# One transformer layer in split fp32: moving the casts of the first feed-forward's up projection, loading the condition row earlier, and keeping two pieces of its down projection

## The chip, the core and the metric

The kernel runs on one core of one Trainium2 chip. The metric is the device time of one execution in microseconds (us), as the median of several runs. Five engines work side by side, each with its own instruction queue: TensorE (PE in the profile; PEld is its weight load), VectorE (DVE), ScalarE (ACT), GpSimd (POOL), and SyncE (SP), which here only issues DMAs. GpSimd issues DMAs too, and a DMA in its queue that has to wait holds back everything behind it.

## The reference, cut to what is computed

Two streams of 256 tokens with 2048 channels: the latent tokens `x` and the context tokens `ctx`. A layer is a SwiGLU half step on both streams, a mixing step (attention of grouped queries beside a Hyena convolution), and a second SwiGLU half step on the latent stream. Each is preceded by an RMS norm with shift, scale and gate from a condition vector through one linear map `w_ada`.

```python
mod   = (silu(c)     @ w_ada + b_ada)[:, None, :]
mod_c = (silu(c_ctx) @ w_ada + b_ada)[:, None, :]

def swiglu(h, w_up, w_down):
    gate, up = split(h @ w_up, 2, axis=-1)
    return (silu(gate) * up) @ w_down          # w_up: 2048 x 11264, w_down: 5632 x 2048

def half_ffn(s, m, slot, g, w_up, w_down):
    h = modulate(rms_norm(s, g), chunk(m, 3 * slot), chunk(m, 3 * slot + 1))
    return s + 0.5 * chunk(m, 3 * slot + 2) * swiglu(h, w_up, w_down)

x   = half_ffn(x,   mod,   0, g_norm[0], w_ffn1_up, w_ffn1_down)
ctx = half_ffn(ctx, mod_c, 0, g_norm[0], w_ffn1_up, w_ffn1_down)
# then: projections of both streams, keys and values first; attention, Hyena, output projection
x   = half_ffn(x, mod, 2, g_norm[2], w_ffn2_up, w_ffn2_down)
```

All data are fp32.

## The kernel before

**Split products.** Every fp32 operand is kept as a high part `hi` (a rounded copy, made by a cast on ScalarE) and a remainder `lo = x - hi` (a subtraction on VectorE). A product is three TensorE instructions, hi·hi, hi·lo and lo·hi (`mm3`, L247 to L249). Weights come in pieces of 512 KB, `raw` tiles with four buffers (`weight_load`, L224); `weight` makes `whi` (cast, L236) and `wlo` (L240), three buffers each.

**The wave.** The first three of the 44 tiles (of 128 columns of gate and 128 of value) of the up projection run side by side while the channels d = 0 to 15 are normalised one after the other (`wave_h`, L872 to L876). Into the same stretch go the rows of `w_ada` for the first shift and scale (`wrow` loads by SyncE, products L190), and the steps of the Hyena filter, whose results `spec` GpSimd stores (L726). Then the three tiles are closed (`close`, L381 is the silu), the condition row goes through GpSimd into a small tile (L955), through silu (L959) and back to memory (L960), and SyncE spreads it over all partitions (`crow`, L968).

**The up projection, tiles j = 3 to 43 (`up`, L490).** Both streams go through at once, 512 columns a product. A tile has four pieces, kq = 0 to 3, of 512 KB. Piece 0 is always "plain": its two halves are cast (L425), the negated high part is written (L426), and the raw piece is added to it by an accumulating DMA on GpSimd's queue (L427), so that VectorE has no part in it; it is loaded by GpSimd (L224) into a pool of one buffer, `plain`. From j = 5 piece 3, from j = 7 piece 2 and from j = 9 piece 1 are "quads": in place of 16 products there are 14 of half the width, of sums of weights and sums of activations. Such a piece is prepared one piece ahead, in this order: cast `bhi` of its plain blocks (ACT, L436), remainder `blo` (DVE, L439), three sums in `raw` (DVE, L442 to L444), cast `whi` of the sums (ACT, L465), remainder `wlo` (DVE, L471). `bhi` and `blo` have two buffers.

**The close of a tile with quads (L516 to L524).** ScalarE copies a part out of PSUM (L516), VectorE forms six sums, ScalarE takes silu (L523), VectorE multiplies (L524), giving the act `u`. Then ScalarE casts the act (L534) and writes the negative (L535), and GpSimd stores both (L536, L537) and later accumulates the act on the second (L270, which is the line of the helper `then`). PSUM banks alternate between PA and PB by tile, so that the next tile starts while one is closed.

**Dots.** The rest of `w_ada` is applied on VectorE as dot products of 1.28 us (L151) of 512 KB loads `adaw` (L141 and L144, SyncE, two buffers) with `crow`. After every piece a hook adds the rate 0.82 to an account and issues a dot for each whole one; hooks start at j = 4.

**The down projection.** Eleven groups of four tiles, in two passes of four pieces dq. The last two groups of the second pass run by halves (`APART`): first the context half (part 1), then the latent half (part 0), both with all pieces dq = 4 to 7 loaded and split; while the latent half runs, the context stream is normalised on VectorE and ScalarE (L342 to L345), and each finished piece is added to the stream (L584). Then comes the projection to keys and values (L1055 to L1057), whose weights go through L236 and L240.

**What sets the order.** The instruction streams are made by a scheduler that follows the order of the code and priorities; `then` and `issue_after` put one instruction behind another in that order.

Of the kernel before, what the change touches and what calls it, by code (L numbers as in the profile page):

```python
# [18 lines left out]
P = 128  # L19
D = 2048  # L20
# [14 lines left out]
ADA_RATES = (0.82, 1.15, 1.42)  # L35
# [27 lines left out]
def hybrid_layer_kernel(ctx: ExitStack, tc: tile.TileContext, a):  # L63
# [296 lines left out]
    class Ffn:  # L360
        def __init__(self, wup, wdown, cm, hook=None):
# [4 lines left out]
            self.held = {}  # L366
            self.sums, self.first, self.begun, self.unadded = {}, {}, None, None
# [50 lines left out]
        def prepare(self, j, kq):  # L418

            pool = adap if kq == 0 and j > WAVE else None  # L420
            raw = weight_load(self.wupq[j - WAVE, kq], (P, 2, 4, P), nc.gpsimd if pool else None, pool)
            if kq == 0:
                hi, lo = ([U((P, 4, P), F32R) for _ in range(2)] for _ in range(2))
                for q in range(2):
                    S.copy(hi[q], raw[:, q])  # L425
                    S.activation(lo[q], hi[q].bitcast(F32), AF.Copy, scale=-1.0)  # L426
                    self.added = nc.gpsimd.dma_start(lo[q], raw[:, q].bitcast(F32R), accum_op=ALU.add)  # L427
                return [(hi, lo)]
            if not self.quads(j, kq):
                return [weight(None, (P, 2, 4, P), raw=raw)]  # L430
            return raw

# [13 lines left out]
        def quad_weights(self, j, kq):  # L446
# [15 lines left out]
            with ExitStack() as order:  # L462
                if cast is not None:
                    order.enter_context(tc.issue_after(cast.ins))
                S.copy(thi, raw)  # L465
# [24 lines left out]
        def up(self, j):  # L490
# [4 lines left out]
            for kq in range(4):  # L495
                w = self.ahead if kq == 0 else self.quad_weights(j, kq) if self.quads(j, kq) else self.prepare(j, kq)
# [30 lines left out]
        def keep(self, j, act):  # L527
# [5 lines left out]
            hi, minus = U((P, 2, L), F32R), U((P, 2, L), F32R)  # L533
            S.copy(hi, act)  # L534
            S.activation(minus, hi.bitcast(F32), AF.Copy, scale=-1.0)  # L535
            nc.gpsimd.dma_start(actd[j][:, 0], hi)  # L536
            nc.gpsimd.dma_start(actd[j][:, 1], minus)  # L537
            self.unadded = j, act
            if j < WAVE:
                self.add_act()  # L540

        def add_act(self):
            if self.unadded:
                j, act = self.unadded
                self.unadded = None
                then(self.added, nc.gpsimd.dma_start, actd[j][:, 1], act.bitcast(F32R), accum_op=ALU.add)
# [16 lines left out]

        def step(self, g, dq, banks, begin, end, part=None, done_=None):
# [387 lines left out]
    for _ in steps:  # L952
        pass
# [729 lines left out]
```

## Time and profile before

| | |
|---|---|
| median of 3 runs | 2630.1 us |
| lowest and highest run | 2628.18, 2631.96 us |
| the profiled execution | 2625.92 us |
| its span | 2624.1 us |
| first close of the wave's tiles (L381) | 150.72 us |
| last close of the up projection (L516) | 1017.61 us |
| second wait of the key/value projection ends (L1056) | 1508.07 us |
| bytes read from HBM, written | 545.10 MB, 38.57 MB |
| mean granted clock of TensorE | 0.997 |

A row of the timeline gives the start, the duration, the engine, the line, the operation, output and inputs, their shapes, and in square brackets the idle time of the engine ahead of it with what ended it. Names without numbers stand for all tiles of that name. Matmuls overlap, so the distance between two starts is their price, not the duration: 0.227 us for 512 columns without a stall. A line number is one of the kernel before unless it is said otherwise.

### The profile page before, as it was taken

To read this page: it belongs to the slowest core of one execution; us is meant where nothing else is said; L and a number is where in the kernel's file an instruction comes from. 1 tells how busy PE (TensorE), PEld (TensorE's weight loads), DVE (VectorE), ACT (ScalarE), POOL (GpSimd) and SP (SyncE) were. 2 spreads that over 40 slices of the span, in tenths; PEclk is the share of its full clock that TensorE was granted. 3 is DMA by queue.
4 is the path that set the end of the run, shared out by engine and by line. 5 is a ranking of instruction groups with operands and counts; after the bars stand their busy time and mean duration, and the time that the engine had idled before them with its cause. 6 is when DMAs were issued, how large, how long until landed. Compare 5 with 4: busy or idle time off the path is not lost.

```text
span 2624.1 us, 38011 instructions
## 1 busy us (share of the span) xinstructions
PE 2592.5 (99%) x14480; PEld 2228.7 (85%) x14480; DVE 1891.7 (72%) x3051; ACT 1115.3 (43%) x1543; POOL 275.2 (10%) x435
## 2 busy tenths in 40 slices
PE   8999999999999999999999999999999999999999
PEld 5678999999999999888888988888788888888887
DVE  6766888888888887777988796888755455554444
ACT  5344444444444443112211555466544444444333
POOL 1121111212212123320010000000000000000000
PEclk9999999999999999999999999999999999999999
DMA  9987888888988889996897566345566555566665
GB/s 368 363 248 220 236 251 246 241 243 240 248 244 256 249 244 316 395 363 208 280 331 241 179 192 186 113 131 175 167 187 191 187 190 189 189 189 208 201 203 154
DMA packets 193925, 607.68 MB, mean 232 GB/s; under 512 B 22316, under 2 KB 25357, under 8 KB 189389
## 3 DMA queue, kind: packets, MB, share of 16 engines
q1 hardware_dynamic: 134684, 483.42, 56.3%
q0 software_dynamic: 58864, 121.69, 17.6%
q8 instruction: 113, 1.85, 0.3%
q14 instruction: 72, 0.58, 0.1%
q10 hardware_dynamic: 192, 0.13, 0.0%
HBM read 545.10 MB, written 38.57 MB: 222 GB/s over the span
## 4 chain that ended last, share of the span: by engine, by line
PE 84%; DVE 6%; DMA 5%; ACT 3%; issue 2%; POOL 0%; SPq 0%; DVEq 0%; ACTq 0%; POOLq 0%
PE pa L1343 10%; PE pa L1342 10%; PE pa L1344 10%; PE pb L247 7%; PE pb L249 7%; PE pb L248 7%; PE pa L247 7%; PE pa L249 7%; PE pa L248 7%; PE pa L255 3%; DMA adaw<-in_w_adaT_dram 2%; PE pa L257 2%; DVE wlo L471 1%; PE pa L1056 1%; PE pa L1057 1%
## 5 line engine op out<-in xcount | busy, mean ns | idle before, releaser
L240 DVE TENSOR_TENSOR wlo<-raw,whi 128x1024 fp32r<-128x1024 f32 x487 | 595.6, 1223 | 476.4 <-ACT whi L236 474.9
L236 ACT CAST whi<-raw 128x1024 fp32r<-128x1024 f32 x487 | 512.4, 1052 | 876.8 <-PE pa L1344 413.4
L1342 PE MATMUL pa<-whi,u 128*128 128x512 f32 x1060 | 413.9, 391 | 0.0
L1343 PE MATMUL pa<-wlo,u 128*128 128x512 f32 x1060 | 412.8, 390 | 0.3 <-DVE wlo L240 0.3
L1344 PE MATMUL pa<-whi,u 128*128 128x512 f32 x1060 | 412.8, 390 | 0.0
L247 PE MATMUL pa<-u,whi 128*128 128x256 f32 (+1 forms) x928 | 311.6, 337 | 2.2 <-ACT u L859 2.1
L249 PE MATMUL pa<-u,wlo 128*128 128x256 f32 (+1 forms) x928 | 309.5, 334 | 2.8 <-DVE wlo L471 2.8
L248 PE MATMUL pa<-u,whi 128*128 128x256 f32 (+1 forms) x928 | 309.2, 333 | 0.4 <-DVE u L864 0.4
L249 PE MATMUL pb<-u,wlo 128*128 128x256 f32 (+1 forms) x920 | 303.6, 330 | 3.1 <-DVE wlo L471 3.1
L247 PE MATMUL pb<-u,whi 128*128 128x256 f32 (+1 forms) x920 | 304.6, 331 | 0.0
L248 PE MATMUL pb<-u,whi 128*128 128x256 f32 (+1 forms) x920 | 302.8, 329 | 0.0
L1343 PEld LDWEIGHTS pa<-wlo,u 128*128 128x128 f32 x1060 | 199.0, 188 | 41.5 <-DVE wlo L240 0.7
L1344 PEld LDWEIGHTS pa<-whi,u 128*128 128x128 f32 x1060 | 199.0, 188 | 41.5
L1342 PEld LDWEIGHTS pa<-whi,u 128*128 128x128 f32 x1060 | 199.0, 188 | 40.7
L151 DVE CUSTOM_DVE_ANT_0 adas<-adaw,crow,cond 128x1024 bf16<-128x1024 f32 x160 | 204.9, 1281 | 11.1 <-DMA adaw<-in_w_adaT_dram 9.4
L151 DVE CUSTOM_DVE_ANT_0 adas<-adaw,crow,mod 128x1024 bf16<-128x1024 f32 x160 | 205.0, 1281 | 7.2 <-DMA adaw<-in_w_adaT_dram 5.1
L247 PEld LDWEIGHTS pa<-u,whi 128*128 128x128 f32 x928 | 176.1, 190 | 25.1 <-issue 4.5
L249 PEld LDWEIGHTS pa<-u,wlo 128*128 128x128 f32 x928 | 176.3, 190 | 21.4 <-DVE wlo L471 4.2
L249 PEld LDWEIGHTS pb<-u,wlo 128*128 128x128 f32 x920 | 174.7, 190 | 20.4 <-DVE wlo L471 4.5
L248 PEld LDWEIGHTS pa<-u,whi 128*128 128x128 f32 x928 | 176.5, 190 | 17.5 <-DVE u L864 1.5
L247 PEld LDWEIGHTS pb<-u,whi 128*128 128x128 f32 x920 | 174.8, 190 | 17.5 <-issue 2.0
L248 PEld LDWEIGHTS pb<-u,whi 128*128 128x128 f32 x920 | 174.8, 190 | 15.8 <-issue 0.4
(357 smaller groups left out, 4654.7 us busy)
## 6 DMA issues: line engine op xcount, KB each, us to landing
adaw<-in_w_adaT_dram SPq DMA_DIRECT2D x224, 512.0 KB, 5.8
raw<-in_w_dn_dram SPq DMA_DIRECT2D x184, 512.0 KB, 4.3
raw<-in_w_up_dram SPq DMA_DIRECT2D x176, 512.0 KB, 3.5
raw<-in_w_up1q_dram SPq DMA_DIRECT2D x124, 512.0 KB, 5.0
u<-act POOLq DMA_DIRECT2D x136, 256.0 KB, 10.9
act<-u POOLq DMA_DIRECT2D x131, 256.0 KB, 5.0
wrow<-in_w_ada_dram SPq DMA_DIRECT2D x32, 1024.0 KB, 9.3
plain<-in_w_up1q_dram POOLq DMA_DIRECT2D x40, 512.0 KB, 6.3
```

The costliest lines, as they stand in the source:

```text
L151: V.tensor_tensor_reduce(out=sc, in0=t, in1=crow[i][:, b * (D // 2) : (b + 1) * (D // 2)], scale=1.0, scalar=mcol if b else bada[:, c * KT ...
L236: S.copy(hi, raw)
L240: last_lo[0] = V.tensor_sub(lo, raw, hi.bitcast(F32))
L247: PE.matmul(ps, w[0], xx[0], start=start, stop=False)
L248: PE.matmul(ps, w[0], xx[1], start=False, stop=False)
L249: return PE.matmul(ps, w[1], xx[0], start=False, stop=stop)
L255: PE.matmul(ps, w[0], x, start=start, stop=stop)
L257: PE.matmul(ps[:, 0, :], w[1], x[:, 0, :], start=False, stop=False)
L471: last_lo[0] = V.tensor_sub(tlo, raw, thi.bitcast(F32))
L1342: PE.matmul(ps[t], hi, w[0], start=start, stop=False)
L1343: PE.matmul(ps[t], hi, w[1], start=False, stop=False)
L1344: last = PE.matmul(ps[t], lo, w[0], start=False, stop=stop)
```

## The change

Three parts.

**1. Casts.** The load of the plain piece is issued one tile earlier, behind the accumulate of the half before it. Its two halves are cast and negated at pieces 1 and 2 of the tile before (`plain_half`), each behind that piece's cast `whi` (`behind_cast`). The act is no longer cast at the close but at piece 3 of the next tile (`store`), again behind that piece's `whi`, with all of its stores and its accumulate, in two tiles of a pool `sg` of three buffers. The acts of the wave are stored at pieces 0, 2 and 3 of tile 3.

**2. Condition row.** The row is loaded at d = 6 of the wave, goes through silu at d = 8, and is spread at d = 14. The hooks issue dots from j = 3 on, at 0.80 instead of 0.82. The loads of ScalarE's function tables rise from 11 to 13 in the program, both new ones in the wave.

**3. Kept pieces.** In the last group of the down projection, pieces dq = 6 and 7 are loaded once, in the context half, and split there in two halves each into general tiles (`U`); the latent half takes them from there.

```diff
-ADA_RATES = (0.82, 1.15, 1.42)
+ADA_RATES = (0.8, 1.15, 1.42)
...
         def prepare(self, j, kq):
-            pool = adap if kq == 0 and j > WAVE else None
-            raw = weight_load(self.wupq[j - WAVE, kq], (P, 2, 4, P), nc.gpsimd if pool else None, pool)
-            if kq == 0:
...
-                for q in range(2):
-                    S.copy(hi[q], raw[:, q])
-                    S.activation(lo[q], hi[q].bitcast(F32), AF.Copy, scale=-1.0)
-                    self.added = nc.gpsimd.dma_start(lo[q], raw[:, q].bitcast(F32R), accum_op=ALU.add)
+        def plain_half(self, j, q):
+            raw = self.plain[0]
+            if q == 0:
+                self.ahead = [tuple([U((P, 4, P), F32R) for _ in range(2)] for _ in range(2))]
+            hi, lo = self.ahead[0][0][q], self.ahead[0][1][q]
+            self.behind_cast(S.copy, hi, raw[:, q])
+            S.activation(lo, hi.bitcast(F32), AF.Copy, scale=-1.0)
+            nc.gpsimd.dma_start(lo, raw[:, q].bitcast(F32R), accum_op=ALU.add)
+            if q == 1 and j >= WAVE + 1:
+                self.plain_load(j + 1, adap)
+
+        def side(self, j, kq):
+            if kq in (1, 2) and j < JT - 1:
+                self.plain_half(j + 1, kq - 1)
+            if self.kept and (kq == 3 or j == WAVE and kq != 1 or j == JT - 1 and kq == 1):
+                self.store(*self.kept.pop(0))
...
-                if kq == 1:
-                    if j < JT - 1:
-                        self.ahead = self.prepare(j + 1, 0)
-                    self.add_act()
+                self.side(j, kq)
                 self.hook()
...
+        def store(self, j, act):
+            hi, minus = (T(up, (P, 2, L), "sg", F32R, 3) for _ in range(2))
+            self.behind_cast(S.copy, hi, act)
             S.activation(minus, hi.bitcast(F32), AF.Copy, scale=-1.0)
+            then(self.plain[1], nc.gpsimd.dma_start, actd[j][:, 0], hi)
             nc.gpsimd.dma_start(actd[j][:, 1], minus)
+            nc.gpsimd.dma_start(actd[j][:, 1], act.bitcast(F32R), accum_op=ALU.add)
...
+            if part is not None and end and dq in PASSES[-1][-2:]:
+                halves = self.kept_weight(g, dq)
+            else:
+                whi, wlo = weight(self.wdown[g, dq], (P, GRP, 2, P))
+                halves = [(whi[:, n : n + 2], wlo[:, n : n + 2]) for n in (0, 2)]
...
+        if d == 6:
+            rows = U((2 * KT, P))
+            nc.gpsimd.dma_start(rows, a["crow"].rearrange("i (k p) -> (i k) p", p=P))
+        if d == 8:
+            S.activation(rows, rows, AF.Silu)
+            nc.gpsimd.dma_start(silu_rows.rearrange("i k p -> (i k) p"), rows)
+        if d == KT - 2:
...
+            row_in(rows_pool, 0)
```

In the order of instructions the change shows at four places; line numbers are those of each kernel. First ScalarE at a close of the stage with quads. Before, around the close that begins with L516 (L534 and L535 are the act, L425 and L426 the plain halves, L436 and L465 the quads' bhi and whi):

```order
L516 COPY sq_3021<-pb_2805 128x256
L465 CAST whi_3076<-raw_2964 128x1024
L523 ACTIVATE sq_3021<-sq_3021 128x512
L534 CAST u_3033<-u_3022 128x512
L535 ACTIVATE u_3034<-u_3033 128x512
L425 CAST u_3128<-plain_3126 128x512
L436 CAST bhi_3145<-raw_3143 128x768
L426 ACTIVATE u_3130<-u_3128 128x512
L425 CAST u_3129<-plain_3126 128x512
L465 CAST whi_3148<-raw_3071 128x1024
L426 ACTIVATE u_3131<-u_3129 128x512
```

The same place now (L534 begins the close, L541 is its silu, L456 bhi, L485 whi; L270 on plain with L438 is a plain half, L270 on u with L557 the act):

```order
L534 COPY sq_2799<-pa_2581 128x256
L270 CAST u_2898<-plain_2714 128x512
L438 ACTIVATE u_2900<-u_2898 128x512
L541 ACTIVATE sq_2799<-sq_2799 128x512
L456 CAST bhi_2909<-raw_2907 128x768
L485 CAST whi_2912<-raw_2843 128x1024
L270 CAST u_2899<-plain_2714 128x512
L438 ACTIVATE u_2901<-u_2899 128x512
L456 CAST bhi_2971<-raw_2969 128x768
L485 CAST whi_2974<-raw_2907 128x1024
L270 CAST sg_3024<-u_2800 128x512
L557 ACTIVATE sg_3025<-sg_3024 128x512
```

The act's pair has moved from ahead of bhi and whi to behind the next whi, one plain half stands ahead of the silu, the other behind whi.

Second, GpSimd's queue at tile 3, before (L270 is an act's accumulate, L536 and L537 its stores, L427 the accumulates of the plain halves):

```order
L270 DMA act_28_108<-u_1556 128x512
L536 DMA act_29_109<-u_1569 128x512
L537 DMA act_29_109<-u_1570 128x512
L536 DMA act_30_110<-u_1579 128x512
L537 DMA act_30_110<-u_1580 128x512
L270 DMA act_29_109<-u_1566 128x512
L427 DMA u_1663<-plain_1659 128x512
L427 DMA u_1664<-plain_1659 128x512
```

And now (L559 and L270 are stores of acts, L560 their accumulates, L439 the plain halves'):

```order
L559 DMA act_29_109<-sg_1694 128x512
L560 DMA act_28_108<-u_1567 128x512
L439 DMA u_1649<-plain_1576 128x512
L560 DMA act_29_109<-u_1570 128x512
L439 DMA u_1650<-plain_1576 128x512
L559 DMA act_30_110<-sg_1737 128x512
L224 DMA plain_1691<-in_w_up1q_dram 128x1024
```

The accumulates of the plain halves stand each behind one act's accumulate.

Third, VectorE at the end of the down projection, before (L584 adds a finished piece, L342 and L345 normalise, the first two L240 are pieces 6 and 7, the third is the projection's first):

```order
L240 TENSOR_TENSOR wlo_15066<-raw_15063,whi_15065 128x1024
L345 SCALAR_TENSOR_TENSOR u_15056<-mt_15057,mod_3_10_87,u_15056 128x256
L584 SCALAR_TENSOR_TENSOR u_13771<-pb_14821,mod_2_7_84,u_13771 128x256 x2
L342 SCALAR_TENSOR_TENSOR mt_15082<-u_11965,mod_4_12_89,u_11129 128x256
L342 SCALAR_TENSOR_TENSOR mt_15099<-u_13769,mod_4_12_89,u_11129 128x256
L240 TENSOR_TENSOR wlo_15108<-raw_15105,whi_15107 128x1024
L345 SCALAR_TENSOR_TENSOR u_15081<-mt_15082,mod_3_10_87,u_15081 128x256
L345 SCALAR_TENSOR_TENSOR u_15098<-mt_15099,mod_3_10_87,u_15098 128x256
L584 SCALAR_TENSOR_TENSOR u_13775<-pb_14822,mod_2_7_84,u_13775 128x256 x2
L342 SCALAR_TENSOR_TENSOR mt_15124<-u_13769,mod_4_12_89,u_11129 128x256
L342 SCALAR_TENSOR_TENSOR mt_15141<-u_13773,mod_4_12_89,u_11129 128x256
L240 TENSOR_TENSOR wlo_15153<-raw_15150,whi_15152 128x1024
```

And now (L610 adds a finished piece):

```order
L342 SCALAR_TENSOR_TENSOR mt_15084<-u_11965,mod_4_12_89,u_11129 128x256
L342 SCALAR_TENSOR_TENSOR mt_15101<-u_13769,mod_4_12_89,u_11129 128x256
L345 SCALAR_TENSOR_TENSOR u_15064<-mt_15065,mod_3_10_87,u_15064 128x256
L610 SCALAR_TENSOR_TENSOR u_13771<-pb_14829,mod_2_7_84,u_13771 128x256 x2
L345 SCALAR_TENSOR_TENSOR u_15083<-mt_15084,mod_3_10_87,u_15083 128x256
L345 SCALAR_TENSOR_TENSOR u_15100<-mt_15101,mod_3_10_87,u_15100 128x256
L342 SCALAR_TENSOR_TENSOR mt_15120<-u_13769,mod_4_12_89,u_11129 128x256
L342 SCALAR_TENSOR_TENSOR mt_15137<-u_13773,mod_4_12_89,u_11129 128x256
L240 TENSOR_TENSOR wlo_15149<-raw_15146,whi_15148 128x1024
```

The wlo of pieces 6 and 7 are gone; that of the projection is the first to follow.

Fourth, ScalarE in the wave at d = 8, now (L988 is silu of the condition row, L900 the activation of channel d, L236 casts of the wave's weights, L197 a step of `w_ada`'s rows):

```order
L197 COPY sg_936<-pb_909 128x256
L236 CAST whi_952<-raw_821 128x1024
L988 ACT_TABLE_LOAD
L988 ACTIVATE u_907<-u_907 32x128
L900 ACTIVATE u_943<-sq_945,mod_6_83 128x256 x2
L236 CAST whi_971<-raw_823 128x1024
L236 CAST whi_987<-raw_825 128x1024
```

Before, the same rows stand there without the two of L988. On GpSimd the condition row's load and store follow the two stores of `spec` (L726 before, L752 now) that are issued ahead of it.

More of the change, by code (lines that the diff above doesn't have):

```diff
@@ L365, in __init__ @@
             self.mm = mm3
-            self.held = {}
-            self.sums, self.first, self.begun, self.unadded = {}, {}, None, None
+            self.held, self.pieces = {}, {}
+            self.sums, self.first, self.begun, self.kept, self.cast, self.plain = {}, {}, None, [], None, None
             self.wupq = a["w_up1q"]
@@ L418, in prepare @@
         def prepare(self, j, kq):
[L420 to L428 removed]
+            raw = weight_load(self.wupq[j - WAVE, kq], (P, 2, 4, P))
             if not self.quads(j, kq):
@@ L464, in quad_weights @@
                     order.enter_context(tc.issue_after(cast.ins))
-                S.copy(thi, raw)
+                self.cast = S.copy(thi, raw)
             if cast is not None:
@@ L562, in fetch, with kept_weight @@
                 self.held[g].append(act)
-        def step(self, g, dq, banks, begin, end, part=None, done_=None):
-            whi, wlo = weight(self.wdown[g, dq], (P, GRP, 2, P))
+        def kept_weight(self, g, dq):
+            if (g, dq) not in self.pieces:
+                raw = weight_load(self.wdown[g, dq], (P, GRP, 2, P))
+                self.pieces[g, dq] = [split(raw[:, 2 * n : 2 * n + 2], (P, 2, 2, P)) for n in range(2)]
+                return self.pieces[g, dq]
+            return self.pieces.pop((g, dq))
+        def step(self, g, dq, banks, begin, end, part=None, done_=None):
+            if part is not None and end and dq in PASSES[-1][-2:]:
[3 more added lines that the diff above has]
+                halves = [(whi[:, n : n + 2], wlo[:, n : n + 2]) for n in (0, 2)]
             for i2 in range(2):
@@ L571, in step @@
                     act = act if part is None else [t[:, part, :] for t in act]
-                    self.mm(ps, (whi[:, jj, i2, :], wlo[:, jj, i2, :]), act, begin and jj == 0 and not (i2 and part is not None),
+                    self.mm(ps, [t[:, jj % 2, i2, :] for t in halves[jj // 2]], act, begin and jj == 0 and not (i2 and part is not None),
                             end and jj == GRP - 1 and (i2 == 1 or part is None))
@@ L979, in hybrid_layer_kernel @@
         f1.up(j)
-        if j == WAVE:
-            f1.hook = lambda: (next(build, None), ada_hook() if done[0] < len(ADA_UP) * KT * 2 else None)
     rs1 = U((P, 2, L))
```

49 lines of the change are left out of this document (22 added, 27 removed).

## The prediction

> **What bounds the kernel now.** I read the page first: the busy shares and the chain that ended last.
>
> ```profile
> PE 2592.5 (99%) x14480; PEld 2228.7 (85%) x14480; DVE 1891.7 (72%) x3051; ACT 1115.3 (43%) x1543; POOL 275.2 (10%) x435
> PE 84%; DVE 6%; DMA 5%; ACT 3%; issue 2%; POOL 0%; SPq 0%; DVEq 0%; ACTq 0%; POOLq 0%
> ```
>
> TensorE is busy 99% and holds 84% of the chain. The change takes no product away, so it can gain only what TensorE loses between products. The view of waits says where that is, the table of stretches how many products go through.
>
> ```profile
> PE pb L249 <- DVE wlo L471: 3.1, 7, 0.8
> PE pa L1056 <- DVE wlo L240: 3.0, 2, 2.5
> PE pa L249 <- DVE wlo L471: 2.8, 5, 0.8
> PE pa L249 <- DMA u<-plain: 2.1, 1, 2.1
> 154.00:176.00 22.00, 22.00 (x98) 18.20 (x97) 13.37 (x22) 11.06 (x17) 8.88 (x13) 1.00 0.99 315
> 176.00:198.00 22.00, 19.91 (x81) 16.01 (x81) 13.51 (x23) 9.36 (x14) 4.84 (x7) 0.92 0.93 244
> 307.34:997.03 689.69, 683.70 (x4952) 648.60 (x4951) 573.07 (x974) 323.67 (x462) 141.23 (x197) 1.00 0.86 246
> ```
>
> Each row of waits gives total, times, longest. In a row of stretches stand the length, the busy time of PE, PEld, DVE, ACT and POOL with counts, the granted clock, the DMA share and GB/s. Three places can be touched.
>
> Place A is the first piece of tile j=4, which waits 2.1 us for the accumulate DMA that makes the plain piece's low half. In the 22 us around it 81 products run, where the 22 us before held 98 of the same size.
>
> Place B is the long stage in which three pieces of each tile are quads. The closes of two tiles that follow each other, and the last such close that I use:
>
> ```profile
> 307.34 0.37 ACT L516 COPY sq<-pb 128x256 f32<-128x256 f32 x1 [1.77 <-PE pb L249]
> 327.92 0.37 ACT L516 COPY sq<-pa 128x256 f32<-128x256 f32 x1 [1.81 <-PE pa L249]
> 997.03 0.37 ACT L516 COPY sq<-pa 128x256 f32<-128x256 f32 x1 [1.81 <-PE pa L249]
> ```
>
> An undisturbed tile takes 327.92 - 307.34 = 20.58 us. From the first close to the last are 33 tiles: 689.69 / 33 = 20.90 us each. The stage loses 33 x 0.32 = 10.6 us. The two waits for wlo L471 show 5.9 of this as idle time; the rest is products that start late around them (ends are modelled, so idle is undercounted). I take the closes for the size, and 5.9 us as the floor of what the stalls are worth.
>
> Place C is the start of the key/value projection, 3.0 us in two waits for wlo L240.
>
> **A: the plain piece of j=4.** What stands in the queues now:
>
> ```profile
> 171.86 0.88 POOL L270 DMA_DIRECT2D act<-u  x1 [4.93 <-DMA act<-u]
> 172.42 2.14 POOL L427 DMA_DIRECT2D u<-plain  x2
> 179.20 0.80 PE L249 MATMUL pa<-u,u 128*128 128x512 f32 x1 [2.09 <-DMA u<-plain]
> 176.01 0.60 ACT L381 ACTIVATE u<-pb 128x512 f32<-128x512 f32 x1 [3.93 <-PE pb L249]
> 201.74 0.60 ACT L381 ACTIVATE u<-pa 128x512 f32<-128x512 f32 x1 [0.27 <-PE pa L249]
> ```
>
> GpSimd's queue issues both accumulates at 172.42, because it waited for the store of an earlier act; they land after TensorE wants them. In the new order the accumulate for half 0 stands behind one act accumulate instead of two, and half 1's behind the next. One 5 us wait in the queue lies between, so half 0 is issued near 172.42 - 4.93 = 167.5 and lands at 172.8 by the median of 5.3 us quoted under B; it is wanted at 179.20 - 2.09 = 177.1, half 1 another 12 products later. The stall goes. Its worth: 17 products missing at 22.00/98 = 0.2245 us give 3.8 us; from close to close, 25.73 - 96 x 0.2245 = 4.2 us. I take 4.0, with 2.1 (the idle alone) as the lower end. By the Trainium skill, "TensorE: Matmul & The Clock Gate", Part 1, the clock falls only after an idle window of about 3.4 us, so this wait should cost its 2.1 us and no more, and the sum would be 1.9 us smaller; the trace disagrees, with a granted clock of 0.92 after 2.09 us.
>
> **B: casts spread over three pieces.** The end of a tile in which TensorE waits, on ScalarE, VectorE and TensorE:
>
> ```profile
> 418.35 0.62 ACT L534 CAST u<-u 128x512 fp32r<-128x512 f32 x1 [1.11 <-DVE u L524]
> 419.54 0.60 ACT L425 CAST u<-plain 128x512 fp32r<-128x512 f32 x1
> 420.05 0.83 ACT L436 CAST bhi<-raw 128x768 fp32r<-128x768 f32 x1
> 420.79 0.63 ACT L426 ACTIVATE u<-u 128x512 fp32r<-128x512 f32 x1
> 421.83 1.04 ACT L465 CAST whi<-raw 128x1024 fp32r<-128x1024 f32 x1
> 422.90 1.23 DVE L471 TENSOR_TENSOR wlo<-raw,whi 128x1024 fp32r<-128x1024 f32 x1 [1.03 <-ACT whi L465]
> 424.19 0.39 PE L249 MATMUL pb<-u,wlo 128*128 128x256 f32 x1 [0.46 <-DVE wlo L471]
> ```
>
> The act's cast and negation, the first half's cast and negation and the second half's cast all stand between the close and whi L465; wlo follows whi, and TensorE waits for wlo. In the new order ScalarE does half 0's pair while VectorE still forms the close's sums (the 1.11 us idle ahead of 418.35), bhi and whi come next, half 1's pair behind whi, the act's pair one piece later. Ahead of this whi the act's pair leaves (418.35 to 419.54, 1.2 us), and half 1's cast (421.83 - 420.79 less the negation that is now earlier, about 0.5 us); the first half's pair moves into idle time (about 1 us). So whi, and wlo with it, comes 1.7 to 2.7 us earlier, against a longest wait of 0.8. What is late next is VectorE: 573.07 of 689.69 us are busy, 83%, and wlo can only be taken when VectorE has finished what its order puts ahead. Its new order has the wlo of the next tile's second piece ahead of the close, and the dots in pairs, of which the second waits for its load:
>
> ```profile
> DVE adas L151 <- DMA adaw<-in_w_adaT_dram: 14.4, 14, 1.8
> ```
>
> 1.8 us at worst is about what the wlo gain in room, so a few tiles should still stall. I take five sixths of 10.6 us, 8.9; the ends are 5.3 (half) and 10.6. ScalarE and VectorE do the same work per tile as before.
>
> The act's two stores and accumulate now stand on GpSimd's queue between the plain halves' accumulates, and the next plain load waits for half 1's landing with the act's store behind it. Cover for that:
>
> ```profile
> 410.50 0.37 ACT L516 COPY sq<-pa 128x256 f32<-128x256 f32 x1 [1.81 <-PE pa L249]
> u<-plain POOLq DMA_DIRECT2D x80, 256.0 KB, 5.3
> DMA to landing us min/median/max: 3.3/5.9/8.8
> ```
>
> whi at 421.83 stands 11.3 us behind the close at 410.50; 2.2 us earlier, and with its 1.04, the cast's 0.60 and the negation's 0.63 us, half 1's negation ends 11.4 us behind the close, and the accumulate is issued near 11.8. It is wanted 20.58 + 12 x 0.2245 = 23.3 us behind that close: 11.5 us of room for a landing of 5.3 (8.8 at most, for this tile's DMAs). Cost nothing; if the cover went, every tile would pay.
>
> **C: pieces 6 and 7 of the last down group kept.**
>
> ```profile
> 1494.69 1.22 DVE L240 TENSOR_TENSOR wlo<-raw,whi 128x1024 fp32r<-128x1024 f32 x1
> 1495.82 0.48 DVE L345 SCALAR_TENSOR_TENSOR u<-mt,mod,u 128x256 fp32r<-128x256 f32 x1
> 1506.80 1.22 DVE L240 TENSOR_TENSOR wlo<-raw,whi 128x1024 fp32r<-128x1024 f32 x1
> 1508.07 0.50 PE L1056 MATMUL pa<-wlo,u 128*128 128x512 f32 x1 [2.49 <-DVE wlo L240]
> ```
>
> The first wlo is that of piece 6; it and piece 7's go, with nothing in their place on VectorE. The next instruction follows such a wlo after 1.13 us (1495.82 - 1494.69), so the projection's second wlo, at 1506.80, comes 2 x 1.13 = 2.26 us earlier. TensorE wanted it at 1508.07 - 2.49 = 1505.58, and 0.5 us sooner once the first wait is gone, 1505.08; it would have it at 1508.07 - 2.26 = 1505.81. So 0.7 of the 3.0 us stay: gain 2.3, ends 0 (the sums of the normalisation, late in the same queue, hold it instead) and 3.0. In the context half the pieces are split in halves: two more instructions on each engine, at the fixed share of a 128x512 against a 128x1024 cast (2 x 0.60 - 1.04 = 0.2 us a piece), hidden by VectorE's and ScalarE's idle there; 0.4 us if not. Two 512 KB loads fewer: nothing, DMA is not what is waited for.
>
> **D: the condition row in the wave.** Here the change adds work on the path. A table load for silu and one back for exp now stand in the wave; the condition row's DMA is waited for by ScalarE.
>
> ```profile
> 149.42 1.28 ACT L381 ACT_TABLE_LOAD   x1
> 150.72 0.60 ACT L381 ACTIVATE u<-pa 128x512 f32<-128x512 f32 x1
> 83.34 1.15 POOL L726 DMA_DIRECT2D spec<-u  x2 [15.89 <-DVE u L723]
> 87.34 0.92 ACT L874 ACTIVATE u<-sq,mod 128x256 fp32r<-128x256 f32 x2 [0.47 <-DVE sq L872]
> 92.50 0.50 PE L247 MATMUL pa<-u,whi 128*128 128x512 f32 x1
> spec<-u POOLq DMA_DIRECT2D x8, 256.0 KB, 7.2
> mt<-in_crow_dram POOLq DMA_DIRECT2D x1, 16.0 KB, 3.1
> 96.11 0.30 POOL L949 COPY mod<-mod 128x1 f32<-128x1 f32 x1 [11.62 <-DVE mod L205]
> ```
>
> The row's load is issued behind the two stores of 83.34, so at 84.5. It lands at 87.6 if it takes the 3.1 us that it takes now in a quieter place, at 91.7 if the stores' 7.2 us. Then come the 1.28 us load and silu (taken at 0.3), and only then the activation of d=8 (0.92 us), which TensorE wants done at 92.50. It may start at 91.6 at the latest; it starts at 89.2 or 93.3. The cost is 0 or 1.7 us; as the row's bytes are few but stand behind the stores, I take 1.0. The copy on GpSimd that waits behind the silu store is due at 96.11, later than both. The return to exp is a second load of 1.28 us, further on; I take nothing for it, and 3 (1.7 and 1.3) as the upper end of the whole. By the Trainium skill, "ScalarE: Activation LUTs", What ACT_TABLE_LOAD costs, each switch costs 2.66 us with its drain and not 1.28, which would add 1.4 us to this cost. The row decides for the smaller: at 149.42 the next instruction starts 1.30 us later, at 150.72.
>
> The dots begin a tile earlier at 0.80 instead of 0.82 a hook: 164 x 0.80 = 131.2 against 160 x 0.82 = 131.2, no dot more or less. Their loads fall into the stretch with a DMA share of 0.99, from which the 1 MB broadcast of the row leaves: nothing.
>
> **Sum.** 4.0 + 8.9 + 2.3 - 1.0 = 14.2 us. The profiled execution took 2625.92 us (span 2624.1), 4.2 below the median of the runs shown, 2630.1; it becomes 2611.7, the median 2615.9. A difference under 0.2% (5.3 us) can hardly be told from none.
>
> **The rivals.**
> 1. VectorE takes ScalarE's place. For it: 83% busy, and the dots in pairs. Against it: wlo waits for whi, not for VectorE's queue, in the rows of B. Half of B and half of C stay: 4.0 + 5.3 + 1.1 - 1.0 = 9.4, 2620.7 us.
> 2. The new order moves casts that were not the cause, or each stall only goes to the next wlo: A alone, 4.0 - 1.0 = 3.0, 2627.1 us, no change by measure. Against it: the casts stand between close and whi.
> 3. Slower: GpSimd's queue. If the accumulate of half 1 lands later than 11.5 us after its issue, because the plain load and the act's stores wait in one queue, each of 39 tiles begins late. At 12.3 us it is 0.8 x 39 = 31.2 us: 2647.1 us. For it: GpSimd waits for such landings already; against it: the longest landing is 8.8.
>
> **How the numbers follow.** Forecast 0.62, rivals 0.18, 0.11 and 0.09. The likeliest is 2615.9. All at its best, 4.2 + 10.6 + 3.0, gives 2612.3, and the runs of before spread 1.9 to a side: low end 2611. Rival 1 with 3 instead of 1 in the wave gives 2622.7, with the same spread 2624.6: high end 2625. That leaves out rivals 2 and 3, 0.20. Faster: 0.62 + 0.18 = 0.80; same 0.11; slower 0.09.
>
> **What would show it.** A: the tile from the close at 176 takes about 21.7 us, and u<-plain is gone from TensorE's waits. B: closes 20.6 to 20.7 us apart on average, waits for the wlo of quads under 1.5 us. C: the second wait of the projection under 1 us. D: a gap before d=8's products of 0 to 2 us. Wrong, if the waits for wlo keep 5 us or more (rival 1 or 2), or if TensorE waits for u<-plain in many tiles (rival 3).

## The result, and the profile after

The changed kernel takes 2675.2 us (median, 2674.2 to 2676.6) where the kernel before took 2631.0 in the runs beside it: a ratio of 1.0165, interval 1.0145 to 1.0184, so 44 us slower where I had forecast 14.2 us faster. The profiled execution's span is 2672.5 us, 48.4 more than before. The page's first line and TensorE's waits in the changed kernel:

```profile
PE 2614.4 (98%) x14480; PEld 2243.2 (84%) x14480; DVE 1896.1 (71%) x3051; ACT 1108.8 (41%) x1545; POOL 275.1 (10%) x435
PE pb L247 <- ACT whi L485: 15.5, 7, 4.5
PE pa L249 <- DVE wlo L491: 10.2, 13, 2.0
PE pb L249 <- DVE wlo L491: 6.9, 11, 0.8
PE pa L247 <- ACT whi L485: 3.3, 4, 1.9
```

The waits for wlo did not shrink, they grew from 5.9 to 17.1 us, and waits for whi came beside them. The wait for u<-plain is gone. The stretch from 310 to 990 us, of before and then of the changed kernel (columns as in the prediction):

```profile
310.00:990.00 680.00, 674.01 (x4881) 639.34 (x4880) 564.60 (x957) 320.18 (x458) 141.09 (x197) 1.00 0.86 245
```

```profile
310.00:990.00 680.00, 645.27 (x4528) 607.87 (x4527) 527.52 (x885) 290.74 (x423) 128.87 (x180) 0.97 0.83 228
```

353 products fewer go through, and VectorE, ScalarE and the DMAs are less busy as well: no engine and no DMA is busier than before, all of them wait more. The closes of the tiles in the timeline (the copy that opens a close, L516 before and L534 now) place the loss. The close of tile 3 stands at 179.93 us instead of 176.01: the wave lost 3.9. Tile 4 then takes 21.76 us instead of 25.73: place A gained 4.0, and at tile 9 both kernels stand at 307.3. From there to tile 43 are 34 tiles, which end at 1067.16 instead of 1017.61: 22.35 us a tile instead of 20.89, a loss of 49.6. Behind the last close 1605.3 us are left instead of 1606.5: place C and the rest gained 1.2.

Whom ScalarE waits for, in the changed kernel:

```profile
ACT u L270 <- DMA act<-u: 162.5, 33, 9.8
ACT u L270 <- DMA plain<-in_w_up1q_dram: 159.5, 33, 6.9
```

Two waits that the kernel before did not have, each once a tile: a cast of a plain half waits for the act's accumulate, and a cast waits for the plain load. The longest tile of the stretch, on ScalarE and then on GpSimd's queue:

```profile
956.46 0.37 ACT L534 COPY sq<-pa 128x256 f32<-128x256 f32 x1
960.59 0.62 ACT L270 CAST u<-plain 128x512 fp32r<-128x512 f32 x1 [3.76 <-DMA plain<-in_w_up1q_dram]
962.30 0.82 ACT L456 CAST bhi<-raw 128x768 fp32r<-128x768 f32 x1
963.03 1.05 ACT L485 CAST whi<-raw 128x1024 fp32r<-128x1024 f32 x1
973.85 0.62 ACT L270 CAST u<-plain 128x512 fp32r<-128x512 f32 x1 [9.78 <-DMA act<-u]
975.04 0.81 ACT L456 CAST bhi<-raw 128x768 fp32r<-128x768 f32 x1
975.76 1.04 ACT L485 CAST whi<-raw 128x1024 fp32r<-128x1024 f32 x1
982.73 0.37 ACT L534 COPY sq<-pb 128x256 f32<-128x256 f32 x1
```

```profile
949.09 0.86 POOL L439 DMA_DIRECT2D u<-plain  x1 [4.00 <-ACT u L438]
954.51 0.56 POOL L224 DMA_DIRECT2D plain<-in_w_up1q_dram  x1 [4.56 <-DMA u<-plain]
955.05 0.55 POOL L270 DMA_DIRECT2D act<-sg  x1
955.59 0.54 POOL L559 DMA_DIRECT2D act<-sg  x1
965.35 0.89 POOL L560 DMA_DIRECT2D act<-u  x1 [9.22 <-DVE mod L164]
965.91 1.24 POOL L439 DMA_DIRECT2D u<-plain  x1
975.42 0.86 POOL L439 DMA_DIRECT2D u<-plain  x1 [8.27 <-ACT u L438]
```

Read these seven rows as a circle. Half 1's accumulate (949.09) must land before the plain load may overwrite its source (954.51). The act's two stores stand behind that load (955.59). The act's accumulate needs the store of the negative to have landed (965.35; the profile puts this wait down to VectorE, whose instruction had long been done; it lasted 9.2 us, and the stores land in 9.1 at the median). Half 1's cast then writes a general tile that this accumulate still reads, and waits for it to land (973.85). Its own accumulate follows at 975.42. The circle took 975.42 - 949.09 = 26.3 us, and the tile it lies in 982.73 - 956.46 = 26.3; the mean tile takes 22.35. A tile of TensorE's work is 20.6. Behind the waiting cast in ScalarE's queue stand bhi and whi, which TensorE needs at once.

### The profile page after: what moved, and what is told of

Its sections match the earlier page's. It is cut to its first block, busy times and chain, and to the rows that moved or that the text cites. A ratio compares the mean times of both kernels' runs of the same rounds, so it can differ in the third digit from the quotient of the medians.

```text
span 2672.5 us, 37860 instructions
## 1 busy us (share of the span) xinstructions
PE 2614.4 (98%) x14480; PEld 2243.2 (84%) x14480; DVE 1896.1 (71%) x3051; ACT 1108.8 (41%) x1545; POOL 275.1 (10%) x435
## 4 chain that ended last, share of the span: by engine, by line
PE 62%; issue 1%; DVE 0%; DMA 0%; ACT 0%; ACTq 0%; DVEq 0%; POOLq 0%
PE pa L1374 10%; PE pa L1372 10%; PE pa L1373 10%; PE pb L247 4%; PE pb L248 4%; PE pb L249 4%; PE pa L255 3%; PE pa L249 3%; PE pa L247 3%; PE pa L248 3%; PE pa L257 2%; PE pa L1086 1%; PE pa L1087 1%; PE pa L1085 1%; PE pb L1529 0%
## 5 line engine op out<-in xcount | busy, mean ns | idle before, releaser
L240 DVE TENSOR_TENSOR wlo<-raw,whi 128x1024 fp32r<-128x1024 f32 x483 | 590.7, 1223 | 469.2 <-ACT whi L236 468.4
L236 ACT CAST whi<-raw 128x1024 fp32r<-128x1024 f32 x483 | 508.2, 1053 | 867.2 <-PE pa L1374 413.4
L247 PEld LDWEIGHTS pb<-u,whi 128*128 128x128 f32 x904 | 176.1, 195 | 34.4 <-ACT whi L485 16.9
L459 DVE TENSOR_TENSOR blo<-raw,bhi 128x768 fp32r<-128x768 f32 x111 | 106.1, 956 | 121.0 <-ACT bhi L456 120.2
```

Source lines behind the costliest of these rows:

```text
L236: S.copy(hi, raw)
L240: last_lo[0] = V.tensor_sub(lo, raw, hi.bitcast(F32))
L247: PE.matmul(ps, w[0], xx[0], start=start, stop=False)
L459: return V.tensor_sub(lo, raw[:, :, 0:3], hi.bitcast(F32))
```

## The experiments

Every kernel is compared with the kernel before on the same chip. That kernel's median was 2630 to 2632 us throughout. Theory loop: the circle is longer than a tile, and wherever it is opened the forecast gain appears. Theory load, the rival: the wait for the plain load at the close is what costs.

**e1, act in its own buffers.** Core of the edit:

```diff
-g, v, u = tmp((P, 2, L)), U((P, 2, L)), T(up, (P, L), "mt", bufs=3)
+g, v, u = tmp((P, 2, L)), T(up, (P, 2, L), "act", bufs=2), T(up, (P, L), "mt", bufs=3)
-return T(up, shape, "u", dt, 58)
+return T(up, shape, "u", dt, 56)
...
             if q == 0:
-                self.ahead = [tuple([U((P, 4, P), F32R) for _ in range(2)] for _ in range(2))]
+                self.ahead = [([None] * 2, [None] * 2)]
+            for part in self.ahead[0]:
+                part[q] = U((P, 4, P), F32R)
```

> The changed kernel with the act that a close leaves in two buffers of its own instead of the general tiles (which go from 58 to 56), and the tiles for each plain half taken when that half is cast. Theory ring: the cast of half 1 waits for a general tile that the act's accumulate still reads, and that accumulate stands behind the act's stores, the plain load and half 1's own accumulate, a loop of 23 to 26 us a tile against 20.6; with the act elsewhere the loop is open, ScalarE's wait for act DMAs (162.5 us) is gone, tiles close about 20.7 us apart, time 2615 to 2625 us. Theory load: ScalarE is held at the close by the plain load's landing (159.5 us of waits), which stays; time 2660 us or more. If both share the loss, in between, near 2645.

Measured: 2669.9 us, ratio 1.0141 (1.0102 to 1.018). The wait of the plain halves' casts for act DMAs is gone, the loss is not. That looked like theory load, but the edit had moved something else too. In most tiles half 0's cast had slid ahead of the close's copy on ScalarE:

```profile
941.73 0.62 ACT L270 CAST u<-plain 128x512 fp32r<-128x512 f32 x1 [3.66 <-DMA plain<-in_w_up1q_dram]
942.25 0.37 ACT L536 COPY sq<-pb 128x256 f32<-128x256 f32 x1
945.69 0.63 ACT L543 ACTIVATE sq<-sq 128x512 f32<-128x512 f32 x1 [2.54 <-DVE sq L541]
947.90 0.62 ACT L270 CAST u<-plain 128x512 fp32r<-128x512 f32 x1
```

Now the close itself waits for the plain load's landing, and half 1's cast comes a whole close later. e10 takes that back.

**e2, stores ahead of the plain load.** One row moves in GpSimd's queue:

```diff
 def plain_half(self, j, q):
 ...
-    if q == 1 and j >= WAVE + 1:
-        self.plain_load(j + 1, adap)
 ...
-def store(self, j, act):
+def store(self, j, act, load):
 ...
-    nc.gpsimd.dma_start(actd[j][:, 1], minus)
+    stored = nc.gpsimd.dma_start(actd[j][:, 1], minus)
+    if load < JT:
+        then(stored, self.plain_load, load, adap)
     nc.gpsimd.dma_start(actd[j][:, 1], act.bitcast(F32R), accum_op=ALU.add)
```

> The changed kernel with the plain load issued behind the act's two stores instead of ahead of them. Theory ring: the stores no longer wait for half 1's accumulate, so the loop is open although the general tiles are still shared; the act's accumulate is issued some 5 us earlier, the wait of half 1's cast shrinks from 4.9 us on average to about 1 or nothing; time 2615 to 2630 us. Theory load: the plain load is not earlier but 1 us later, so ScalarE's wait at the close grows; time 2675 us or more.

Measured: 2613.5 us, ratio 0.9938 (0.9923 to 0.9952): some 62 us less than the changed kernel, 17 less than before, and a little under the range that I had expected. The same stretch, GpSimd's queue over a tile, and ScalarE's wait that theory load blames:

```profile
310.00:990.00 680.00, 680.00 (x4955) 648.25 (x4954) 581.11 (x973) 323.70 (x462) 139.93 (x196) 1.00 0.88 248
751.26 0.86 POOL L439 DMA_DIRECT2D u<-plain  x1 [3.88 <-ACT u L438]
755.64 0.56 POOL L270 DMA_DIRECT2D act<-sg  x1 [3.52 <-ACT sg L270]
756.30 0.55 POOL L557 DMA_DIRECT2D act<-sg  x1
756.92 0.53 POOL L224 DMA_DIRECT2D plain<-in_w_up1q_dram  x1
762.50 0.89 POOL L560 DMA_DIRECT2D act<-u  x1 [5.04 <-DVE raw L461]
771.84 0.86 POOL L439 DMA_DIRECT2D u<-plain  x1 [4.66 <-ACT u L438]
ACT u L270 <- DMA plain<-in_w_up1q_dram: 125.8, 34, 4.9
```

The stores wait for their cast alone, half 1's accumulates come 20.58 us apart, and TensorE has no idle time left in the stretch. The wait for the plain load is still 125.8 us and costs nothing, since bhi and whi behind it have the room. Theory load falls.

**e3, condition row as before; e4, casts as before.** e3 takes part 2 back (row loaded after the wave, dots from tile 4 at 0.82); e4 keeps parts 2 and 3 and takes part 1 back.

> The changed kernel with the condition row as before (after the wave, dots from tile 4 at 0.82). If the wave's loss is the row's landing and the table loads, the close of tile 3 returns from 179.9 to about 176, ScalarE's wait of 4.1 us in front of silu is gone and the time falls by 3.9 us to about 2671. If the wave lost its 3.9 us to the casts of part 1 that now stand behind it, the time stays at 2675. The loop in the later tiles is untouched under every theory.

Measured: 2675.7 us, ratio 1.0177 (1.0158 to 1.0196), no difference to the changed kernel by the time. The expected 2671 was missed. In the trace the close of tile 3 came back to 176.75, 3.2 us earlier, as expected, but at the last close only 1.8 us of it are left (1065.37 instead of 1067.16). From tile 9 on the tiles took 1.4 us more in all than in the changed kernel; no run settles whether that is more than the spread of these tiles from run to run.

> The kernel before with the early condition row and the kept pieces, but the casts of plain pieces and acts as before. All theories of the loss place it in the spread casts: tiles close 20.9 us apart again. Wave +3.9, place A unchanged or +0, place C -2.3 (forecast) or about -1: time 2631 to 2633 us. If the early row or the kept pieces take part in the loss, more than 2640.

Measured: 2626.5 us, ratio 0.9988 (0.9978 to 0.9998), where 2631 to 2633 was expected. So part 1 alone holds the loss. The close of tile 3 is at 179.84, tile 4 has its stall of 2.4 us back, and from tile 9 to 43 the tiles took 706.7 us, 3.6 less than in the profiled execution of before. I had not expected that gain; whether it is from the earlier dots or from how those stalls vary from run to run, no run settles.

**e5, row loaded at d = 2; e6, e2 with the row as before; e7, e2 without the kept pieces.**

```diff
-        if d == 6:
+        if d == 2:
             rows = U((2 * KT, P))
```

> e2 (plain load behind the act's stores) with the condition row's load taken at d = 2 instead of d = 6; silu then goes ahead of the first exp, so that only one table load more than before is left. If the wave loses its 4.6 us in e2 to the wait for the row's landing (3.7 us on ScalarE) and not to the table loads, the close of tile 3 comes back from 180.6 to 177 or less and the time falls to 2609 to 2611 us. If the table loads were the cost, it stays at 2613.

Measured: 2616.8 us, ratio 0.9945 (0.9933 to 0.9957); the close of tile 3 at 179.90. A miss. The store of the silu'd row went ahead as well, waited 15 us on GpSimd's queue, and the filter's loads behind it came late (the first at 58.11 us, at 41.74 in the changed kernel):

```profile
42.10 0.51 POOL L986 DMA_DIRECT2D u<-in_crow_dram  x1
57.61 0.51 POOL L989 DMA_DIRECT2D silu_rows<-u  x1 [14.99 <-ACT u L988]
PE pb L190 <- DVE u L719: 3.2, 1, 3.2
```

The loss changed its place, not its size.

> e2 with the condition row as before (after the wave, dots from tile 4 at 0.82). The wave should get its 4 us back, as in e3, where the close of tile 3 stood at 176.8: 2609 to 2611 us, faster than e2 by 3 to 4 us. If the earlier dots are worth something in the long stage (e4 closed its tiles 3.6 us sooner in all than before), 2613 us or no difference to e2.

Measured: 2610.1 us, ratio 0.9923 (0.991 to 0.9936), the fastest version; the close of tile 3 at 176.50. The early row costs more than it brings: in all 13 kernels that have it this close stands at 179.8 to 183.0, in the three without it at 176.0 to 176.8.

> e2 without the kept pieces: the last group's pieces 6 and 7 are loaded and split in both halves, as before. Forecast's term C: e2 plus 2.3 us, 2616 us, with 3 us of waits for wlo L240 in the key/value projection back. By the spans behind the last close of the up projection (1606.5 before, 1605.0 in e2) it is 1.5 us: 2615.

Measured: 2617.8 us, ratio 0.9949 (0.9937 to 0.9961). Its wave, the same as e2's in the code, happened to be 2.4 us slower; behind the last close 1606.3 us are left, 1.3 more than in e2, and the 3.0 us of waits for wlo L240 are back. Against e2 term C is 1.3; why it isn't more stands under C below.

**e8 to e10 and e13, the links one by one.** e8 is e1 with the act's accumulate moved behind the next plain load; e9 is e8, and e10 is e1, with half 0's cast held behind the close's copy; e13 is e9 with three act buffers.

In e8, e9 and e13:

```diff
-nc.gpsimd.dma_start(actd[j][:, 1], act.bitcast(F32R), accum_op=ALU.add)
+self.unadded.append((j, act))
...
+if kq == 2 and self.unadded:
+    for i, act in self.unadded:
+        then(self.plain[1], nc.gpsimd.dma_start, actd[i][:, 1], act.bitcast(F32R), accum_op=ALU.add)
```

In e9, e10 and e13, around the cast of a half:

```diff
+if q == 0 and self.copied is not None:
+    order.enter_context(tc.issue_after(self.copied.ins))
```

> e1 (act in its own buffers) with the plain load ahead of the act's stores, as in the changed kernel, but the act's accumulate moved behind the next tile's plain load. Theory ring, closed twice (in the queue, where half 0's and half 1's accumulates stand behind the act's accumulate, and in the shared tile): both links are open now, tiles close 20.6 us apart and the time is 2612 to 2618 us, although the stores still wait for half 1's accumulate. If only the stores' place behind the plain load matters, whatever the rest, it stays near e1, 2665 us or more.

Measured: 2649.6 us, ratio 1.0079 (1.0062 to 1.0095). Neither answer.

> e8 (act in its own buffers, its accumulate behind the next plain load, stores still behind the plain load) with the cast of half 0 held behind the close's first PSUM copy on ScalarE, where e8 had it ahead of that copy. Theory: e8's rest of the loss (2649 us) is the copy and VectorE's sums waiting for the plain load's landing behind that cast, not the loop: tiles close 20.6 us apart, time 2612 to 2618 us. If the stores behind the plain load cost something by themselves, 2640 us or more.

Measured: 2640.3 us, ratio 1.0036 (1.0021 to 1.0052). A miss: the copy's place was part of it, but something was left.

> e1 (act in its own buffers, accumulate ahead of the next tile's halves) with half 0's cast held behind the close's copy, as in e9. Theory: one of the loop's two links is left, the one in GpSimd's queue, and one is enough: tiles close 22 us apart or more, time 2650 to 2675 us. If the shared tile was the only link, and e1 was slow by the place of the cast, 2612 to 2620 us.

Measured: 2617.6 us, ratio 0.9943 (0.9925 to 0.9962). My expectation was wrong, and the sum that I had not made says why. With the act elsewhere the circle runs through GpSimd's queue only: half 1's accumulate waits there for the issue of the act's accumulate, and no longer for its landing. The rows of e10 for landings in the stretch from 310 to 990 us, both halves and both stores together:

```profile
act<-sg POOLq DMA_DIRECT2D x66, 256.0 KB, 7.4
u<-plain POOLq DMA_DIRECT2D x66, 256.0 KB, 7.0
```

Each DMA of the circle taken by itself, the medians are 7.8 us for half 1's accumulate to land, 1.7 until the negative's store is issued behind the plain load and the other store, 7.9 for that store to land, 0.5 until the act's accumulate is issued, and 1.1 for it and half 0's ahead of half 1's: 19.0 us, less than a tile. With the landings of the changed kernel (below) it is 17.0, so it should have been expected. This circle cost nothing while it was shorter than the period.

> e9 (2640 us) with three buffers for acts instead of two (general tiles 55). In e9 a close's first write to the act waits for the late accumulate of the act two tiles before. Theory loop: that wait closes another loop, through plain load, act accumulate (8.4 us), the close's sums, half 1's cast and its accumulate; with a third buffer it is open and the time is 2612 to 2620 us. If e9 is slow because four DMAs in a row land later, whatever waits for them, it stays at 2635 us or more.

Measured: 2612.9 us, ratio 0.9934 (0.9917 to 0.995). In e9 VectorE waited at the close for a free act buffer, once a tile:

```profile
DVE act L546 <- DMA act<-act: 112.0, 33, 6.2
```

In e13 no such row is left. So e9's late accumulate, with two buffers, had closed another circle; that is shown, since the third buffer, taken from the general tiles, is the only edit between them. The stores stand behind the plain load in e10 and e13 too, whose tiles take 20.61 and 20.58 us: that place alone costs nothing.

**e12, one store ahead; e14, no accumulate.**

In e12 the plain load stands between the stores, where e2 has it behind both; in e14, made from the changed kernel, the accumulate is left out:

```diff
+stored = then(self.plain[1], nc.gpsimd.dma_start, actd[j][:, 0], hi)
+if load < JT:
+    then(stored, self.plain_load, load, adap)
+then(self.plain[1], nc.gpsimd.dma_start, actd[j][:, 1], minus)
```

```diff
-nc.gpsimd.dma_start(actd[j][:, 1], act.bitcast(F32R), accum_op=ALU.add)
```

> e2 with the plain load between the act's two stores, one row further ahead in GpSimd's queue: the high part's store ahead of it, the store of the negative behind. The accumulate waits for the negative's store, so the loop is closed again by this one row: 2660 to 2680 us, as the changed kernel. If what counts is the number of stores that wait, or the time of the plain load, about half of the loss: 2630 to 2645 us.

Measured: 2630.3 us, ratio 1.0001 (0.9981 to 1.002), with runs from 2617 to 2640: 17 of the 62 us that the changed kernel loses against e2. The circle is closed, as expected, but shorter than I had expected. In the stretch from 310 to 990 us, of the changed kernel and then of e12:

```profile
u<-plain POOLq DMA_DIRECT2D x60, 256.0 KB, 5.6
act<-sg POOLq DMA_DIRECT2D x60, 256.0 KB, 9.1
act<-u POOLq DMA_DIRECT2D x30, 256.0 KB, 5.0
```

```profile
u<-plain POOLq DMA_DIRECT2D x65, 256.0 KB, 6.0
act<-sg POOLq DMA_DIRECT2D x64, 256.0 KB, 6.4
act<-u POOLq DMA_DIRECT2D x33, 256.0 KB, 4.2
ACT u L270 <- DMA act<-u: 84.0, 33, 3.6
```

(The last row is from the waits of the whole of e12.) These medians mix both halves and both stores, so I take each DMA of the circle by itself. In the order of the circle: half 1's accumulate lands, the negative's store is issued, it lands, the act's accumulate is issued, it lands, and cast, negation and issue of the next half 1 follow. The medians are 4.0 + 1.7 + 9.7 + 0.5 + 5.0 + 1.6 = 22.5 us in the changed kernel, whose tiles took 22.35, and 5.5 + 1.1 + 7.8 + 0.5 + 4.2 + 1.6 = 20.7 in e12, whose tiles took 20.92: about a tile of TensorE's work (20.6). So e12 sits at the limit, ScalarE still waits for the act's accumulate once a tile, and the tiles take from 19.5 to 24.5 us.

> The changed kernel without the acts' accumulate DMAs, all else the same, in the same order. It leaves out the act's low part, so its output is another. Theory loop: half 1's cast waits for the landing of the accumulate (5 us) that itself waits for the negative's store (9.1 us); without it the wait in front of half 1's cast is gone, tiles close 20.6 us apart, time 2612 to 2620 us. If the order of stores and plain load holds back something else than that tile, 2650 us or more.

Measured: 2612.8 us, ratio 0.9932 (0.9917 to 0.9946). The order of stores and plain load is that of the changed kernel; without the one DMA that half 1's cast waited for, the loss is gone, and TensorE's 680.00 us of the stretch hold 4955 products as in e2.

**e11, no silu.** e2 with `AF.Copy` in place of `AF.Silu` for the condition row.

> e2 with silu of the condition row replaced by a copy, so the two added table loads are gone, while the row's load is waited for at the same place. It leaves out the silu of the condition, so its output is another. If the landing is the wave's cost, the close of tile 3 stays at 180 us or above and the time at 2612 to 2614; if the table loads are, the close falls to about 178 and the time to 2611.

Measured: 2617.4 us, ratio 0.9948 (0.993 to 0.9966); the close of tile 3 at 182.97. Both table loads are gone and nothing is gained. The time alone would not show it, since the same wave differed by 2.4 us between e2 and e7, but the trace does. ScalarE in the changed kernel, then in e11:

```profile
86.25 1.05 ACT L236 CAST whi<-raw 128x1024 fp32r<-128x1024 f32 x1 [0.97 <-PE pa L248]
87.31 1.28 ACT L988 ACT_TABLE_LOAD   x1
92.68 0.31 ACT L988 ACTIVATE u<-u 32x128 f32<-32x128 f32 x1 [4.08 <-DMA u<-in_crow_dram]
92.89 0.89 ACT L900 ACTIVATE u<-sq,mod 128x256 fp32r<-128x256 f32 x2
```

```profile
93.66 0.31 ACT L988 ACTIVATE u<-u 32x128 f32<-32x128 f32 x1 [5.09 <-DMA u<-in_crow_dram]
```

The table load runs ahead of the landing, inside the wait: it was free, and without it the wait is no shorter. Counted product by product, between 83 and 101 us of the kernel before TensorE falls behind it by 3.4 us in the changed kernel, by 3.0 in e2, by 5.3 in e11 and by 0.1 in e6. The load back to exp, at 109.69 in the changed kernel, adds nothing: TensorE's lag is 3.8 us ahead of it and behind it. So the landing is the cost.

## Why the prediction was wrong

**What bounds the kernel: right.** TensorE's losses were at A, B and C, and e2, e10, e13 and e14 bring the tiles of B to 20.6 us.

**A: right.** 4.0 forecast; tile 4 takes 21.76 us, 3.97 less. The two accumulates are issued at 165.51 and 168.94 in place of 172.42, and the wait is gone. The clock row was the better guide than the idle time alone.

**B: the term was right for the intention, and the step that guarded it failed.** With the loop open B gives 10.6 us: 34 tiles in 699.7 us in e2 (308.00 to 1007.68), in 710.3 before. The prediction took 8.9. What failed is the line "Cost nothing; if the cover went, every tile would pay", the cost of the act's stores and accumulate in GpSimd's queue: it cost 22.35 - 20.58 = 1.8 us a tile, more than the gain. Two sentences ahead of it did not hold. "What is late next is VectorE": it was not; late next was the tile that half 1's cast writes. I followed queues and never asked which buffer a moved cast would get, although the act, kept one piece longer and accumulated later, now held one of eight general tiles that rotate (of the 58, two for each of 16 inputs and three for each of six pairs' sums are held). The second is "the accumulate is issued near 11.8": I read a time from ScalarE's order. It was issued 13.7 to 19.0 us behind the close in the tiles of the stretch (at 975.42, behind the close at 956.46, in the one shown). And "Cost nothing" looked at one link, the landing against its use. That cover even held, as TensorE nowhere in these tiles waits for u<-plain; late were bhi and whi behind the waiting cast. What had to be added up was the circle: a landing, a load, a store, a landing, an accumulate, a landing, back to the cast: 22.5 us against 20.6.

I also did not price the plain load's landing at the close, though its issue behind half 1's landing stood in the order. That wait came (159.5 us); in e2 it was free (125.8 us), which was luck, and in e1, with the close's copy behind it, it was not.

**C: right, where the clock held.** 2.3 forecast, 1.2 to 1.3 measured by the spans behind the last close. The waits did go: 3.0 us before, 0.3 in the changed kernel. But in e2 the 10 us that follow run at a granted clock of 0.83, without a wait of TensorE. The first two rows are of e2, the third is the same stretch in e13, whose last close stands at the same 1007.68 us:

```profile
1494.99 0.50 PE L1086 MATMUL pa<-wlo,u 128*128 128x512 f32 x1 [0.29 <-DVE wlo L240]
1498.88:1508.88 10.00, 10.00 (x42) 8.25 (x42) 7.04 (x13) 3.20 (x6) 0.00 (x0) 0.83 0.67 204
1498.88:1508.88 10.00, 10.00 (x48) 8.12 (x48) 8.64 (x17) 4.08 (x9) 0.00 (x0) 1.00 0.69 212
```

Six products of 0.227 us are 1.4 us. The first product behind the keys' and values' first stretch (L1152 before) starts 533.3 us behind the last close in the kernel before and in e7, 532.1 in e2, and 530.7 to 530.8 in e5, e6, e9, e13 and e14, whose clock holds there: C brings 2.5 us with the clock at 1.00, and half of that where it falls, as it does in the profiles of 8 of the 14 kernels that keep the pieces, the changed one among them. Why it falls there stays open: from 1493 to 1501 us the products of e2 and e13 start at the same times, to 0.05 us. By the Trainium skill ("TensorE: Matmul & The Clock Gate", Part 1) the clock falls after an idle window of about 3.4 us; the trace of e2 has none there, the longest wait being 0.29 us.

**D: the first wait was right, what follows it was not priced.** 1.0 forecast, 3 as the upper end; 3.9 measured in the changed kernel, 3.2 to 4.1 by taking it back (e3, e6). The changed kernel's load of the row, and TensorE's wait for the activation of d = 8:

```profile
84.87 0.51 POOL L986 DMA_DIRECT2D u<-in_crow_dram  x1
PE pa L247 <- ACT u L900: 0.8, 1, 0.8
```

The row's 16 KB landed 92.68 - 84.87 = 7.8 us after issue: the stores' 7.2 us were the right row, not the 3.1 of a quieter place. The 1.28 us table load, which the sum puts behind the landing, had run before it. So the activation began at 92.89, 1.3 us later than the 91.6 that the sum allowed, and TensorE waited 0.8 us for it: a gap of 0 to 2 us, as forecast. The rest of the loss came behind it. On ScalarE whi stood behind silu too, VectorE waited 3.55 us for the activation with wlo and the filter's steps behind it, and TensorE's products fell further back, from 1.3 us behind the kernel before at that product to 3.8 at the one that starts at 100.11 there. The prediction followed one consumer of a queue that serves several. The Trainium skill ("ScalarE: Activation LUTs", What ACT_TABLE_LOAD costs) gives 2.66 us for a switch; no such price shows here, as e11 loses no less without both switches.

**The sum, and luck.** By the spans of the profiled executions e2 is 11.4 us shorter than the kernel before: 4.0 of A, 10.6 of B, 1.4 behind the last close, less 4.6 in the wave. The 17 us of its median are more because the profiled execution of before was shorter than most (2625.92 us, medians of 2630 to 2632). That e2's 2613.5 us lie near the 2615.9 forecast is luck in part. Two slips of the arithmetic change nothing: five sixths of 10.6 are 8.8, not 8.9, and 2612.3 less 1.9 is 2610.4, not 2611.

**Rival 3 was the right place with the wrong point.** It had GpSimd's queue, the plain load and the act's stores in it, at 0.09 and 2647 us. It asked whether a landing takes over 11.5 us, and found 8.8. No landing has to be slow: the median ones add up to 22.5 us in a circle. GpSimd's wait of the plain load for u<-plain in the profile of before (153.7 us, 39 times) was the first link.

## What to carry to other kernels

When work is moved to a later place in a pipeline, write down the circle that it closes (who frees the buffer that it writes, what that waits for, through which queue, back to itself) and add up its issues and landings, each DMA by itself, against one period: here waits of 125.8 us were free with the circle open (e2), and with it at 22.5 us against 20.6 every tile paid the difference. Buffers that rotate in a pool are links of such circles even if no data passes between their users. In a queue of DMAs, what waits for an earlier landing goes last where the circle is near the period: here one row put behind two others turned 44 us lost into 17 us won, and into 22 with the condition row left where it was (e6).

## What the runs showed of the hardware

The landing of a DMA differed with what was issued around it. The store of the act's negative landed in 4.9 us at the median of the stretch from 310 to 990 us in the kernel before, where it stands several us behind the 512 KB load (7.9 and 9.8 in two tiles from 599 us on), in 9.7 right behind that load in the changed kernel, and in 6.0 ahead of it in e2. Both stores together took 7.4 to 10.0 us in the other kernels of that order (e1, e8 to e10, e13, e14). The condition row's 16 KB took 3.1 us after the wave and 7.8 in it. The first was a term of the circle, the second of D, and both were larger in the place to which the change had moved them.

The granted clock fell without a wait that explains it: in e2 it stood at 0.50 from 1501.10 to 1504.50 us, in e13, with the same products at the same times just ahead of it, it did not fall.
